# Two plain groups of the feed-forward network ahead of the products, single PSUM banks, and modulation sums in the plain chunks

## The chip, the cores and the metric

One core of one Trainium2 chip runs the program; nothing is shared with other cores. The metric is device time in microseconds, median of the runs. TensorE is written as PE, VectorE as DVE, ScalarE as ACT, GpSimd as POOL and SyncE as SP.

## The reference, cut to what matters

The program runs two blocks of two layers each. Every layer ends with a gated feed-forward network (FFN) between a modulation and a residual add:

```python
def swiglu(h, w_in, w_out):
    g, u = jnp.split(h @ w_in, 2, axis=-1)
    return (jax.nn.silu(g) * u) @ w_out
...
mod = silu_c @ ada_w[l] + ada_b[l]          # shifts, scales and gates of a layer
...
h = h + g2 * swiglu(modulate(h, norm2_g[l], sh2, sc2), ffn_w_in[l], ffn_w_out[l])
```

The model width is 1024, the hidden width 2816, which is 22 chunks of 128. In the first layer of each block the 512 tokens of the sequence and the 256 of the context go through the FFN together: 768 columns. All is float32. The modulation vectors of the second layer (`silu_c @ ada_w[1]`) depend on no activation, so they can be summed at any time before that layer.

## The kernel before

**Numbers.** TensorE multiplies in a rounded float32 format, so each operand is kept as a high part and a low part, and each product is three matmuls: high x high, high x low, low x high (`mm3`, lines 307, 309, 311, and `mmh`, lines 357 to 359). The high part is a cast on ACT, the low part a subtraction: for weights on POOL (line 300 for 1024 columns, line 349 for 512), for activations mostly on DVE (line 336 in `split`).

**The FFN over 768 tokens** (`ffn`, called in the first layer of each block; the second layers use `ffn_plain`, which the diff does not touch). It goes over the hidden chunks in groups (`FGROUPS[0]`: nine groups of two, then one of four).

- The group of chunks 0 and 1 is computed plainly: gate and up of a chunk are eight mm3 each over 768 columns into a PSUM tile `pd` of 1024 columns, of which there are three. The first three of these (gate 0, up 0, gate 1) run over the operands as they are modulated (lines 597, 598 and 578).
- The other 20 chunks (`pair`) are computed by 7 products of half width (384 columns) instead of 8, in the manner of Strassen's method: sums of halves of the operand (`half_sums`, lines 389 to 394, with casts on line 376 and low parts on line 377, made once, in `hid` tiles and with the halves of x overwritten) and sums of halves of the weights (lines 779 to 782), with the seven results combined by adds (line 770) out of PSUM tiles `sb`, of which there are four, one bank each.
- The down projection of a group (`down`) runs as a generator between the products of the next group. Each of its eight blocks of output rows goes into `sf`, a PSUM tile of 1024 columns of which there is one, in two segments of 512 and 256 columns; `residual_add` (line 642, DVE) scales each segment and adds it to `h`. The next block waits for both.
- `down_last` takes the last group of four.

**Modulation sums** (`ada`). A step is one DMA of 512 KB (a `wraw` tile, of which there are four, shared with the weights) and one or two `scalar_tensor_tensor` on DVE (line 440) that multiply it with a condition vector and accumulate; the first 16 of 48 steps have two. The one that writes its product to `junk` comes first, a second one writes over `wraw`. `fill.pace()` takes 1.3 steps at each call after a pause of five calls, so 45 steps are spread over the chunks, and `down_last` drains the other three.

**Order.** Each engine runs its instructions in the order in which they are placed, and SP issues nearly all DMAs in the same way. The code above sets the order in which work is written; a list scheduler moves it within limits on each engine.

## Time and profile before

| | us |
|---|---|
| median of 3 runs | 4068.76 (4065.93 to 4074.28) |
| profiled execution | 4067.65 |
| its span | 4065.9 |
| PE busy | 3624.0 (89%) |
| DVE busy | 2675.9 (66%) |
| ACT busy | 1455.8 (36%) |
| POOL busy | 1675.6 (41%) |

The profile is one execution. Times of rows are counted in microseconds from the start of its span. A matmul's duration includes the time that it overlaps with its neighbours, so the distance of two starts is what one costs. A wait is read from the idle time of an engine ahead of an instruction and the event that ended it. [...]

### The profile page before, as it was taken

Reading aid. Unit: us, or ns where it says so; the run is one execution under the profiler, and the core shown is the slowest. Engines: PE = TensorE matmul, PEld = TensorE weight load, DVE = VectorE, ACT = ScalarE, POOL = GpSimd, SP = SyncE. Lnnn points to the kernel's source line nnn. Section 1 sums busy time; section 2 is a strip of 40 time slices with the busy share of each in tenths; the row PEclk is TensorE's granted clock in tenths of the full one; section 3 lists DMA queues with packets and bytes.
Section 4 is the critical chain, followed back from the end, with each engine's and each line's share of the span. In section 5 each row is a group of like instructions: output and inputs, shape, how many; then the busy total and the mean of one; then the engine's idle time right before and its main releaser. Section 6 shows DMA issues by size and latency. Waiting matters only on the chain. (4 is left out here: it accounts for less than half of the span.)

```text
span 4065.9 us, 57730 instructions
## 1 busy us (share of the span) xinstructions
PE 3624.0 (89%) x22329; PEld 3065.1 (75%) x22329; DVE 2675.9 (66%) x4827; ACT 1455.8 (36%) x2609; POOL 1675.6 (41%) x1024
## 2 busy tenths in 40 slices
PE   6989889999789899988977879679999899989997
PEld 4777778998677777877756667578898777778886
DVE  4784588877776677746767654778887754464225
ACT  4542222223366322233332322332222355543222
POOL 2112355655322444432332225565555642245443
PEclk9999989999899999989986869889999899999998
DMA  5124123434111255424545767213333322122231
GB/s 193 37 95 157 45 72 110 135 125 137 57 30 45 93 171 176 153 89 120 141 130 158 233 184 260 81 32 114 120 125 121 99 67 65 60 73 78 94 99 57
DMA packets 263010, 450.21 MB, mean 111 GB/s; under 512 B 63504, under 2 KB 168592, under 8 KB 259664
## 3 DMA queue, kind: packets, MB, share of 16 engines
q1 hardware_dynamic: 257536, 424.50, 33.3%
q10 hardware_dynamic: 5200, 22.02, 1.6%
q8 instruction: 176, 2.88, 0.3%
q14 instruction: 98, 0.80, 0.1%
HBM read 383.02 MB, written 63.44 MB: 110 GB/s over the span
## 5 line engine op out<-in xcount | busy, mean ns | idle before, releaser
L300 POOL TENSOR_TENSOR wlo<-wraw,whi 128x1024 fp32r<-128x1024 f32 (+2 forms) x326 | 740.8, 2274 | 1362.3 <-ACT whi L299 1253.0
L307 PE MATMUL pd<-s,whi 128*128 128x512 f32 (+1 forms) x1881 | 644.5, 370 | 38.0 <-ACT s L577 9.5
L299 ACT CAST whi<-wraw 128x1024 fp32r<-128x1024 f32 (+2 forms) x334 | 321.4, 964 | 989.3 <-PE pd L309 471.6
L309 PE MATMUL pd<-s,whi 128*128 128x512 f32 (+1 forms) x1821 | 628.2, 369 | 14.6 <-DVE s L578 6.2
L311 PE MATMUL pd<-s,wlo 128*128 128x512 f32 (+1 forms) x1881 | 637.9, 365 | 1.6 <-POOL wlo L300 1.6
L349 POOL TENSOR_TENSOR wlo<-wraw,whi 128x512 fp32r<-128x512 f32 x240 | 377.9, 1591 | 264.9 <-ACT whi L348 264.9
L307 PEld LDWEIGHTS pd<-s,whi 128*128 128x128 f32 x1881 | 341.6, 194 | 104.2 <-issue 14.0
L357 PE MATMUL sb<-s,whi 128*128 128x384 f32 x1120 | 378.3, 338 | 15.1 <-ACT s L376 11.9
L309 PEld LDWEIGHTS pd<-s,whi 128*128 128x128 f32 x1821 | 332.6, 193 | 74.5 <-DVE s L578 10.1
L358 PE MATMUL sb<-s,whi 128*128 128x384 f32 x1120 | 378.3, 338 | 10.8 <-DVE s L377 6.2
L311 PEld LDWEIGHTS pd<-s,wlo 128*128 128x128 f32 x1881 | 342.4, 193 | 56.1 <-POOL wlo L300 3.5
L359 PE MATMUL sb<-s,wlo 128*128 128x384 f32 x1120 | 376.8, 336 | 0.0
L440 DVE SCALAR_TENSOR_TENSOR junk<-wraw,cond 128x1024 bf16<-128x1024 f32 x160 | 275.0, 1719 | 112.8 <-DMA wraw<-in_ada_w 112.3
L348 ACT CAST whi<-wraw 128x512 fp32r<-128x512 f32 x240 | 139.6, 618 | 409.3 <-PE sb L358 299.6
L357 PEld LDWEIGHTS sb<-s,whi 128*128 128x128 f32 x1120 | 212.2, 190 | 25.1 <-ACT s L376 14.3
L358 PEld LDWEIGHTS sb<-s,whi 128*128 128x128 f32 x1120 | 211.9, 189 | 15.4 <-DVE s L377 9.4
L359 PEld LDWEIGHTS sb<-s,wlo 128*128 128x128 f32 x1120 | 211.8, 189 | 0.0
L307 PE MATMUL sf<-hid,whi 128*128 128x512 f32 x576 | 154.8, 349 | 50.9 <-DVE h L642 50.9
L1149 DVE TENSOR_REDUCE negm<-sc 128x1 f32<-128x512 f32 (+1 forms) x128 | 96.1, 754 | 117.3 <-PE sc L1330 106.5
L642 DVE SCALAR_TENSOR_TENSOR h<-sf,mod,h 128x512 f32<-128x512 f32 (+1 forms) x288 | 163.7, 607 | 10.8 <-PE sf L311 10.8
L642 DVE SCALAR_TENSOR_TENSOR h<-pd,mod,h 128x512 f32<-128x512 f32 (+1 forms) x163 | 105.3, 658 | 89.0 <-PE pd L311 88.7
L309 PE MATMUL sf<-hid,whi 128*128 128x512 f32 x576 | 150.7, 342 | 1.8 <-DVE hid L336 1.8
(414 smaller groups left out, 7886.1 us busy)
## 6 DMA issues: line engine op xcount, KB each, us to landing
wraw<-in_ada_w SPq DMA_DIRECT2D x160, 512.0 KB, 3.5
wraw<-in_ffn_w SPq DMA_DIRECT2D x132, 512.0 KB, 3.5
wraw<-in_ffn_w_in SPq DMA_DIRECT2D x88, 512.0 KB, 3.5
wraw<-in_ffn_w_out SPq DMA_DIRECT2D x44, 512.0 KB, 3.6
recd<-xr SPq DMA_DIRECT2D x72, 256.0 KB, 2.9
rec<-recd ACTq DMA_DIRECT2D x12, 1536.0 KB, 7.9
rec<-recd SPq DMA_DIRECT2D x12, 1536.0 KB, 7.0
raw<-in_ada_w SPq DMA_DIRECT2D x32, 512.0 KB, 5.8
```

Of the source, the lines that this page charges most:

```text
L299: nc.scalar.copy(hi, raw)
L300: (lo_eng or nc.gpsimd).tensor_tensor(out=lo, in0=raw, in1=hi.bitcast(F32), op=ALU.subtract)
L307: nc.tensor.matmul(ps[:, o:o + b - a], lhsT=whi, rhs=xhi[:, a:b], start=start, stop=False)
L309: nc.tensor.matmul(ps[:, o:o + b - a], lhsT=whi, rhs=xlo[:, a:b], start=False, stop=False)
L311: nc.tensor.matmul(ps[:, o:o + b - a], lhsT=wlo, rhs=xhi[:, a:b], start=False, stop=stop)
L348: nc.scalar.copy(hi[:, r], src)
L349: nc.gpsimd.tensor_tensor(out=lo[:, r], in0=src, in1=hi[:, r].bitcast(F32), op=ALU.subtract)
L357: mm(ps, lhsT=hi[:, k], rhs=a, start=i == 0, stop=False)
L358: mm(ps, lhsT=hi[:, k], rhs=b, start=False, stop=False)
L359: mm(ps, lhsT=lo[:, k], rhs=a, start=False, stop=i == 3)
L440: nc.vector.scalar_tensor_tensor(raw if r else self.junk, raw, 1.0, self.cond[r], op0=ALU.mult, op1=ALU.mult, accum_out=m[:, j, r:r + 1])
L642: nc.vector.scalar_tensor_tensor(h[k][:, x:y], ps[:, x - o:y - o], m[:, g + k, r:r + 1], h[k][:, x:y], op0=ALU.mult, op1=ALU.add)
```

## The change

- Two groups are computed plainly, chunks 0 to 3. The down projection of group 0 is drained after chunk 2, with its blocks in `pd` tiles, one tile for each segment; that of group 1 runs between the first products.
- `half_sums` is called after chunk 1; its last part, which overwrites halves of x (operands `t3`), is split off into `rest()`, called after the plain chunks.
- Modulation steps: four after each of chunks 1, 2 and 3, two at every second block of the plain down, so 20 steps with 36 sums ahead of the products; then one at every second block of the later downs. `pair` has none and `down_last` none left.
- PSUM for the products is three `sb` tiles and three `sf` tiles of one bank each. A block of the down projection takes one `sf` tile for 512 columns and one for 256, each with six matmuls in a row and an evacuation of its own.
- In `pair` the low part of `hid` is computed on POOL (line 802) instead of DVE; the high part stays on ACT (line 801).

Lines move by two or more: 440 is 442 after, 578 is 580, 597 and 598 are 599 and 600, 642 is 644, 770 is 773, 779 to 782 are 782 to 785, 794 and 795 are 797 and 798, 810 is 815 (the plain chunk's product of silu and up).

```diff
--- before.py
+++ after.py
@@ -399,9 +399,11 @@
             ops["t1"].append(put(half(), y1[:, a], G))
             ops["t4"].append(put(half(), y2[:, a], V))
             t3.append((h1, l1, t))
-        for i, (h1, l1, t) in enumerate(t3):
-            ops["t3"].append(put((h1[:, b], l1[:, b]), t, (V, G)[i % 2]))
-        return ops
+        def rest():
+            for i, (h1, l1, t) in enumerate(t3):
+                ops["t3"].append(put((h1[:, b], l1[:, b]), t, (V, G)[i % 2]))
+
+        return ops, rest
 
 
     def ada_start(self, l, block):
@@ -703,7 +705,7 @@
         es = self.es
         hp = es.enter_context(self.tc.tile_pool(name=self.nm("hid"), bufs=8, reuse_waits="tile"))
         sp = es.enter_context(self.tc.tile_pool(name=self.nm("half"), bufs=1, reuse_waits="tile"))
-        BUFS.update(hid=8, s3=1, up=1, sb=4, sf=1)
+        BUFS.update(hid=8, s3=1, up=1, sb=3, sf=3)
         H = n // 2
         ha, hb = slice(0, H), slice(H, n)
         oi = 0
@@ -716,7 +718,7 @@
             done(f, ps, a, b)
             st.add(h[f], a, b)
 
-        def down(hid):
+        def down(hid, tag="sf", pace=1):
 
             nonlocal oi
             nk = len(hid)
@@ -726,12 +728,13 @@
                 hl = self.wload(wo(oi))
                 oi += 1
                 for f in range(nf):
-                    ps = self.ps("sf")
-                    for kc in range(nk):
-                        self.mm3(ps, *hl[f * nk + kc], xs[0][kc], xs[1][kc], kc == 0, kc == nk - 1, self.segs(n))
-                    done(f0 + f, ps, 0, n)
-                    if f == nf - 1:
-                        fill.pace()
+                    for a, b, o in self.segs(n):
+                        ps = self.t(self.pp, [P, 1024 if tag == "pd" else 512], tag)
+                        for kc in range(nk):
+                            self.mm3(ps, *hl[f * nk + kc], xs[0][kc], xs[1][kc], kc == 0, kc == nk - 1, [(a, b, 0)])
+                        self.residual_add(h, ps, f0 + f, m, g, a, b, o)
+                    if f % 2:
+                        fill.step(pace)
                     yield
 
         def down_last(hid):
@@ -793,27 +796,35 @@
             add(sl[:, hb], sl[:, hb], product(g2, "b2"))
             A.activation(sl, sl, AF.Silu)
             V.tensor_tensor(out=sl, in0=sl, in1=up, op=ALU.mult)
-            fill.pace()
             between.step()
-            return self.split(sl, n, pool=hp)
-
+            hi, lo = (self.t(hp, [P, T], "hid", F32R)[:, :n] for _ in range(2))
+            A.copy(hi, sl)
+            nc.gpsimd.tensor_tensor(out=lo, in0=sl, in1=hi.bitcast(F32), op=ALU.subtract)
+            return hi, lo
+
+        hids = [[], []]
         with ExitStack() as e1:
             self.psum(e1, pd=3)
             first = self.chunks([wg(0), wu(0), wg(1)], x, n, parts=parts or self.parts(n))
             self.flush()
-            hid = []
-            for c in range(2):
-                pg = first[2 * c]
+            for c in range(4):
+                pg = first[2 * c] if c < 2 else self.chunk(wg(c), x, n)
                 pu = first[1] if c == 0 else self.chunk(wu(c), x, n)
                 sl = self.s()
                 nc.scalar.activation(sl[:, :n], pg[:, :n], AF.Silu)
                 nc.vector.tensor_tensor(out=sl[:, :n], in0=sl[:, :n], in1=pu[:, :n], op=ALU.mult)
-                hid.append(self.split(sl, n, pool=hp))
-                fill.pace()
-        ops = self.half_sums(x, n, hp)
+                hids[c // 2].append(self.split(sl, n, pool=hp))
+                if c == 1:
+                    ops, rest = self.half_sums(x, n, hp)
+                if c:
+                    fill.step(4)
+                if c == 2:
+                    Fill(down(hids[0], "pd", 2)).drain()
+        rest()
+        hid = hids[1]
         with ExitStack() as e2:
-            self.psum(e2, sb=4, sf=1)
-            for grp in FGROUPS[0][1:]:
+            self.psum(e2, sb=3, sf=3)
+            for grp in FGROUPS[0][2:]:
                 between = Fill(down(hid))
                 hid = [pair(c, between) for c in grp]
                 between.drain()
```

DVE while the operands of the first FFN are modulated, before:

```order
L597 TENSOR_TENSOR s_3947<-h_3569,s_3504 128x512
L514 SCALAR_TENSOR_TENSOR st_r_3993<-rs_t_3996,st_r_3993 128x2
L598 TENSOR_SCALAR s_3947<-s_3947,modA_3817,mod_23_112 128x512
L578 TENSOR_TENSOR s_3951<-s_3947,s_3950 128x512
L597 TENSOR_TENSOR s_3954<-h_3632,s_3504 128x512
L598 TENSOR_SCALAR s_3954<-s_3954,modA_3817,mod_23_112 128x512
L597 TENSOR_TENSOR s_3961<-h_3695,s_3504 128x512
L598 TENSOR_SCALAR s_3961<-s_3961,modA_3817,mod_23_112 128x512
L578 TENSOR_TENSOR s_3965<-s_3961,s_3964 128x512
L597 TENSOR_TENSOR s_3968<-h_3746,s_3504 128x512
L598 TENSOR_SCALAR s_3968<-s_3968,modA_3817,mod_23_112 128x512
L597 TENSOR_TENSOR s_3975<-h_3778,s_3504 128x512
```

and after, with sums of line 442 between the modulation (599, 600) and the product (580) that PE multiplies:

```order
L442 SCALAR_TENSOR_TENSOR junk_419,mod_831_4055<-wraw_4378,cond_413 128x1024
L515 TENSOR_TENSOR rs_t_3996<-rs_t_3996,rs_h_3995 128x2
L599 TENSOR_TENSOR s_3947<-h_3569,s_3504 128x512
L516 SCALAR_TENSOR_TENSOR st_r_3993<-rs_t_3996,st_r_3993 128x2
L442 SCALAR_TENSOR_TENSOR wraw_4378,mod_831_4055<-wraw_4378,cond_416 128x1024
L514 TENSOR_TENSOR rs_t_3996<-st_r_3993 128x2
L600 TENSOR_SCALAR s_3947<-s_3947,modA_3817,mod_23_112 128x512
L515 TENSOR_TENSOR rs_t_3996<-rs_t_3996,rs_h_3995 128x2
L442 SCALAR_TENSOR_TENSOR junk_419,mod_831_4055<-wraw_4382,cond_413 128x1024
L516 SCALAR_TENSOR_TENSOR st_r_3993<-rs_t_3996,st_r_3993 128x2
L580 TENSOR_TENSOR s_3951<-s_3947,s_3950 128x512
L599 TENSOR_TENSOR s_3954<-h_3632,s_3504 128x512
```

In the whole stretch there are 12 such sums ahead of the last line 580 in the first FFN, and 4 in the second.

ACT at the end of the half sums, before (after the casts comes the first copy out of a product):

```order
L376 CAST s_3950<-hid_4338 128x384
L376 CAST s_4345<-hid_4337 128x384
L376 CAST s_4351<-hid_4337 128x384
L376 CAST s_4365<-hid_4355 128x384
L777 COPY s_4388<-sb_4389 128x384
L376 CAST s_3957<-hid_4338 128x384
L376 CAST s_4351<-hid_4356 128x384
L376 CAST s_4365<-hid_4356 128x384
```

and after, where the silu of chunk 2's gate (line 814, `pd_4392`) stands behind the casts of line 376:

```order
L376 CAST s_4315<-hid_4320 128x384
L376 CAST s_4344<-hid_4335 128x384
L376 CAST s_4329<-hid_4320 128x384
L376 CAST s_4344<-hid_4336 128x384
L376 CAST s_4350<-hid_4336 128x384
L376 CAST s_4364<-hid_4354 128x384
L814 ACTIVATE s_4496<-pd_4392 128x768
L376 CAST s_4350<-hid_4355 128x384
L335 CAST hid_4499<-s_4496 128x768
```

The silu was not there before, since chunk 2 was made by products. The third tile of the plain down takes the buffer of chunk 2's up, which DVE's line 815 reads; that comes after the two lines 644 of the first block.

POOL at the end of a group, before:

```order
L300 TENSOR_TENSOR wlo_6119<-wraw_6116,whi_6118 128x1024
L349 TENSOR_TENSOR wlo_6139<-wraw_6072,whi_6138 128x512
L349 TENSOR_TENSOR wlo_6139<-s_1122_6076,whi_6138 128x512
L349 TENSOR_TENSOR wlo_6189<-wraw_6073,whi_6188 128x512 x2
L349 TENSOR_TENSOR wlo_6239<-wraw_6072,whi_6238 128x512
```

and after, with the low part of the group's second `hid` behind the down weights (line 300) and two parts of the next chunk's weights:

```order
L300 TENSOR_TENSOR wlo_6161<-wraw_6158,whi_6160 128x1024
L349 TENSOR_TENSOR wlo_6182<-wraw_6114,whi_6181 128x512
L349 TENSOR_TENSOR wlo_6182<-s_1150_6118,whi_6181 128x512
L802 TENSOR_TENSOR hid_6111<-s_5907,hid_6110 128x768
L349 TENSOR_TENSOR wlo_6236<-wraw_6115,whi_6235 128x512 x2
L349 TENSOR_TENSOR wlo_6287<-wraw_6114,whi_6286 128x512
```

The low part of `hid`, which stood on DVE, now stands behind three instructions of POOL; for the first chunk of a group it stands behind the down weights alone.

## Rows read from the trace of the kernel before

**Rows 1.** The page, engine totals: busy us, share of the span, instructions.
```profile
PE 3624.0 (89%) x22329; PEld 3065.1 (75%) x22329; DVE 2675.9 (66%) x4827; ACT 1455.8 (36%) x2609; POOL 1675.6 (41%) x1024
```

**Rows 2.** Stretches by line 357, first FFN: us, busy (instructions), clock, DMA.
```profile
574.20:626.50 52.30, 19.04 (x56) 10.79 (x57) 0.97 0.35 111
...
731.70:779.50 47.80, 18.75 (x56) 10.54 (x57) 1.00 0.42 133
...
971.00:1002.40 31.40, 18.84 (x56) 10.50 (x56) 1.00 0.53 163
```

**Rows 3.** The same, second FFN.
```profile
2757.50:2809.00 51.50, 18.73 (x56) 10.49 (x57) 1.00 0.34 113
...
3154.00:3184.20 30.20, 18.71 (x56) 10.48 (x56) 1.00 0.52 159
```

**Rows 4.** PE's waits, 574 to 1002: total us, times, longest.
```profile
PE sf L307 <- DVE h L642: 19.8, 18, 2.5
```

**Rows 5.** Stretches, all engines: PE, PEld, DVE, ACT, POOL busy, clock, DMA.
```profile
503.00:534.00 31.00, 18.28 (x67) 14.12 (x67) 25.94 (x30) 9.46 (x19) 21.06 (x13) 0.67 0.05 17
...
574.00:731.00 157.00, 144.19 (x790) 134.76 (x789) 136.82 (x189) 42.52 (x66) 86.17 (x48) 0.97 0.36 114
```

**Rows 6.** PE's waits, 503 to 537.
```profile
PE sb L357 <- ACT s L376: 7.6, 2, 4.8
PE sb L358 <- POOL s L377: 2.3, 2, 1.7
```

**Rows 7.** Timeline, PE: start, duration, engine, line, tiles, count.
```profile
497.69 0.51 PE L307 MATMUL pd<-s,whi 128*128 128x512 f32 x2
...
498.74 0.51 PE L307 MATMUL pd<-s,whi 128*128 128x512 f32 x2
...
822.24 0.34 PE L357 MATMUL sb<-s,whi 128*128 128x384 f32 x1
...
822.76 0.33 PE L357 MATMUL sb<-s,whi 128*128 128x384 f32 x1
```

**Rows 8.** Line 440, 400 to 1040: ns minimum/median/maximum, first and last start.
```profile
L440 DVE SCALAR_TENSOR_TENSOR junk<-wraw,cond x48: 1208/1226/2317, 546.9 to 988.9; 128x1024 bf16<-128x1024 f32 x48
...
L440 DVE SCALAR_TENSOR_TENSOR wraw<-wraw,cond x16: 1211/1842/2355, 548.5 to 711.9; 128x1024 f32<-128x1024 f32 x16
```

**Rows 9.** Timeline, DVE, half sums.
```profile
503.10 0.95 DVE L810 TENSOR_TENSOR s<-s,pd 128x768 f32<-128x768 f32 x1 [2.13 <-PE pd L311]
...
510.75 0.94 DVE L390 TENSOR_TENSOR hid<-s,s 128x768 f32<-128x768 f32 x1
...
529.73 1.35 DVE L391 TENSOR_TENSOR hid<-hid 128x384 f32<-128x384 f32 x1
```

**Rows 10.** Timeline, all engines, end of a group.
```profile
823.92 1.13 DVE L642 SCALAR_TENSOR_TENSOR h<-sf,mod,h 128x512 f32<-128x512 f32 x2
...
824.15 0.34 PE L359 MATMUL sb<-s,wlo 128*128 128x384 f32 x1
...
825.11 0.61 PE L307 MATMUL sf<-hid,whi 128*128 128x512 f32 x2 [0.62 <-DVE h L642]
825.51 2.94 POOL L300 TENSOR_TENSOR wlo<-wraw,whi 128x1024 fp32r<-128x1024 f32 x1 [3.13 <-ACT whi L299]
...
828.41 2.02 POOL L349 TENSOR_TENSOR wlo<-wraw,whi 128x512 fp32r<-128x512 f32 x1
...
829.30 0.84 ACT L335 CAST hid<-s 128x768 fp32r<-128x768 f32 x1 [0.73 <-DVE s L795]
...
830.38 2.01 POOL L349 TENSOR_TENSOR wlo<-s,whi 128x512 fp32r<-128x512 f32 x1
...
831.52 0.51 PE L307 MATMUL sf<-hid,whi 128*128 128x512 f32 x2
```

**Rows 11.** POOL's sum of operand parts, line 389: ns minimum/median/maximum.
```profile
L389 POOL TENSOR_TENSOR hid<-s,s x4: 1832/2032/2293, 505.9 to 527.4; 128x768 f32<-128x768 f32 x4
```

## The prediction

> **What bounds the kernel now.** I read the page's engine totals first: TensorE is busy 89% of the span [rows 1], so over the whole program only matmul work or idle TensorE time can move the end. The diff touches the two feed-forward networks over 768 tokens (about 455 to 1002 us, and 2640 to 3184 us), so I cut these into stretches by the matmuls of the 7 products, 28 of the first kind to a chunk. [...] In the first network a group of two chunks takes 52.3 us at first and 47.8 us later [rows 2]; the second starts at 51.5 [rows 3]. The table of waits says what is idle: from 574 to 1002 us `sf` waits 19.8 us for line 642, the residual add that empties its only buffer [rows 4]. In the early groups VectorE is the late one: busy 136.8 of 157 us [rows 5]. [...]
>
> **The change part by part, matmul work.** In the plain chunk three pairs (512 + 256 columns) take 498.74 - 497.69 = 1.05 us, and 16 such triples make a chunk: 16.7 us. Three matmuls of a product take 822.76 - 822.24 = 0.52, so a product of 12 is 2.08 and a chunk of 7 is 14.6 [rows 7]. Two more plain chunks in each network therefore cost 4.2 us each, 8.4 in all; this is inside the walk below. The comparison stands where the same work is left, the last 18 chunks by products: before at 574.2 and 2757.5 us.
>
> **The plain part, first network.** A modulation sum takes 1.23 us (median) in the form that writes `junk`, 1.84 in the one that writes `wraw` and 1.21 at best, with 0.08 for the accumulator [rows 8]; I take 1.31 each. The order puts 12 of them among the modulation of the operands ahead of its last product (line 578, now 580), where VectorE works nearly without a gap before. 12 x 1.31 = 15.7; two weight sums of 0.68 leave the place, four gaps of 0.69 behind ScalarE are filled, and about a microsecond of slack goes: +10.5. What stood at 503.1 us (the last plain product, [rows 9]) comes at 513.6. Then silu x up, one sum and the low part: the half sums start at 518.5. TensorE has the new chunk 2 (16.7 us) and the first down tile to do, until 531.5.
>
> Here the order makes a new wait. The down projection of group 0 goes through the three `pd` buffers, two of which hold gate and up of chunk 2. The second down tile needs the gate's buffer, freed by ScalarE's silu, which is queued behind the casts of the half sums; these wait for VectorE's line 391 of the last quarter. Before, from the first line 390 to the end of that line 391 is 510.75 to 531.1 = 20.3 us [rows 9], of which 1.9 is work of others; now four sums (5.2) and an evacuation (0.7) stand in it: 24.4, so 542.9, and with the silu 543.8. TensorE idles 12 us at the second tile, and 2.4 more at the third, which needs the up buffer behind two VectorE steps. The rest of the down is VectorE's: 7 evacuation pairs of 1.13 [rows 10], 3 us of half sums, a low part and four sums are 17.8, to 565.5. The weights of chunk 3 share the ring of four with the modulation loads and follow VectorE's sums: I put 3 us on it, about two sums. Chunk 3 is 16.7, its first columns at a lower clock 2: the products start at 588, **14 us later** than 574.2. Meanwhile eight more sums (10.5) lie under chunk 3 and cost nothing; without that cover they would be 10.5.
>
> Bounds: if TensorE never waits in the down, it is 12 + 2.4 earlier, so 0; if every sum takes 1.84 as in the slower form, the some 20 on this path add 0.6 each, so 26. In the second network the order has only 4 sums ahead of line 580, but 8 instead of 4 among the evacuations: the first term falls from 10.5 to some 0 to 4, the last grows by 5: **+9** (bounds -3 and 21).
>
> **The stretch by products.** Late groups of 47.7 still hold some 0.62 us of wait per chunk (as [rows 10] show at 825.11), so without any they are 46.4. Eight groups of 46.4 and the last two chunks at 29.5 (14.6 each, and the gaps between) are 400.7, where before 574.2 to 1002.4 is 428.2 [rows 2] and 2757.5 to 3184.2 is 426.7 [rows 3]: a gain of 27.5 + 26 = 53.5. Three reasons let me take it whole: a buffer is free when the third last tile is emptied; the 32 steps of one sum each come to 28, one to every second block; and the low part of `hid` leaves VectorE.
>
> But the low part goes to GpSimd, and there it costs. Before, at a group's end, the last product ends at 824.5; GpSimd does the next down weights (825.51, 2.94) and two weight parts (828.41, 830.38), to 832.4; `hid` hi starts on ScalarE at 829.30 and its low part on VectorE is done before `sf` starts at 831.52 [rows 10]. Now line 802 stands behind those two weight parts. GpSimd's nearest operation, two inputs of 768 columns, takes 1.83 to 2.29, median 2.03 [rows 11]: it would end at 834.4, 9.9 after the last product. TensorE has an `sf` pair and two products in between (6.25) and 0.92 of the new `sf` until it reads that part: at 7.2. If all four operations run at their shortest, it lands 0.7 late, with these durations 2.7. I take 1.8, since VectorE, which is busy beside GpSimd, has less to do. Seven downs in each network follow a group's end so: 14 x 1.8 = 25 (bounds 10 and 38). For first chunks of a group there is slack of a whole chunk: nothing.
>
> The split evacuations cost VectorE the same 512 + 256; six 512-column matmuls before six of 256 instead of alternating cost TensorE under 0.12 a chunk, in the 46.4. Clock lost after the longer holes: an estimate of 3 in all (the clock was 0.67 in such a stretch, [rows 5]), bounds 0 and 8.
>
> **Sum**, against the profiled 4067.65 us (span 4065.9; the median is 1.1 higher): +14 + 9 - 53.5 + 25 + 3 = -2.5, so 4065 beside that run, **4067 us** beside the median of 4068.76. It is a change of no size that comes from two terms of 25 to 50.
>
> **The rivals.** *Hidden backlog.* ScalarE's casts come early enough, so the second down tile finds its buffer: the half sums are through by 531. For it speaks that some of the half-sum chain was waiting for GpSimd (line 377, [rows 6]), into which sums fall free. Against it, VectorE was busy 25.9 of 31 us [rows 5]. It would save 14 in each network: 4039. *Low part on time.* If GpSimd's weight parts run ahead, the 25 are not lost: 4042. For it, GpSimd idles 3 us ahead of the down weights at 825.51 [rows 10]; against it, it waits there for ScalarE's cast, which stays where it is.
>
> *Sums at the slow rate* (slower). The sum that writes `wraw` has 1.21 at best and 1.84 in the middle, 2.36 at worst [rows 8], with the same size: something beside it slows it, and GpSimd is the engine that is busy 21 of 31 us there [rows 5]. If the some 20 sums on the path take 1.84 + 0.08 instead of 1.31, each network loses 12: 4091. It decides from a mean of 1.6 in the plain part. [...]
>
> *Banks that free nothing* (slower). If the early `sf` waits are VectorE's lateness and not the single buffer, three small banks only put them off: a bank holds one segment, so three hold 1.5 of the old tiles. Half of the 53.5 would go: 4094. Against it, the early groups shrink from 52.3 to 47.8 us once the steps carry one sum [rows 2], with one buffer all the while.
>
> **How the numbers follow.** My forecast has 0.36 (own range 4056 to 4078), hidden backlog 0.20, low part on time 0.12, slow sums 0.22, banks that free nothing 0.10. A measurement of this kernel tells about 0.2% from no change, that is 4060.6 to 4076.9. Faster: 0.20 + 0.12 + 0.05 of the forecast's lower end = 0.37; within: 0.28; slower: 0.22 + 0.10 + 0.03 = 0.35. The range 4038 to 4096 leaves out both gains together, and slow sums together with a low part 2.7 late.
>
> **What would show it.** In the profile after: the first product of chunk 4 at about 588 and 2767 us; a wait of `pd` for ScalarE's silu of some 12 us in each down of group 0; `sf` waiting for line 802 some 1 to 3 us, 14 times, and hardly for line 644; groups of two chunks at 46.4 to 48.5 from the first on; and some 36 modulation sums at a mean near 1.3 us ahead of the first product. The forecast is wrong if the wait for the silu is missing, or if line 802 is never waited for (both faster), or if the sums' mean passes 1.6 or `sf` still waits for VectorE (both slower).

## The result, and the profile after

| | before | after |
|---|---|---|
| median, us | 4067.98 (4 runs, 4065.93 to 4074.28) | 4115.67 (4 runs, 4112.12 to 4120.63) |
| span of the profiled execution, us | 4065.9 | 4114.3 |

The ratio is 1.0115, 95% interval 1.0098 to 1.0133: the change makes the kernel 48 us slower. The forecast was 4067 with a range of 4038 to 4096.

The page of the changed kernel has the engine totals (beside [rows 1]) and, among the costliest groups, a wait that did not exist before (columns: busy and mean ns | idle before it and what ended it):

```profile
PE 3646.1 (89%) x22377; PEld 3082.9 (75%) x22377; DVE 2607.7 (63%) x4747; ACT 1443.5 (35%) x2585; POOL 1683.8 (41%) x1040
...
L309 PE MATMUL sf<-hid,whi 128*128 128x512 f32 (+1 forms) x512 | 175.6, 343 | 30.1 <-POOL hid L802 30.1
```

DVE has 68 us less to do, and PE 22 us more. 30.1 us of idle PE end with POOL's line 802.

**Where the time went.** The stretches of the first network by products, all engines (us; busy PE, PEld, DVE, ACT, POOL; granted clock as a share of full speed):

```profile
596.70:644.70 48.00, 47.99 (x264) 45.40 (x265) 29.30 (x47) 12.02 (x19) 21.17 (x16) 0.97 0.37 110
...
696.50:748.30 51.80, 48.39 (x267) 45.24 (x266) 34.43 (x50) 13.79 (x22) 27.72 (x19) 0.97 0.32 102
...
898.40:946.60 48.20, 46.43 (x267) 43.85 (x266) 30.72 (x47) 15.71 (x24) 28.70 (x19) 1.00 0.34 110
```

And of both networks by line 357 alone, the last two chunks and, in the second, the first group (us; PE, PEld; clock):

```profile
994.20:1029.30 35.10, 19.58 (x56) 10.87 (x56) 0.95 0.25 76
...
2801.20:2849.20 48.00, 19.64 (x57) 11.20 (x57) 0.96 0.33 110
...
3199.10:3234.20 35.10, 19.44 (x56) 10.84 (x56) 0.95 0.26 76
```

The bounds of these stretches are the account, beside [rows 2, 3]. The 18 chunks by products start at 596.7 instead of 574.2 us: **+22.5**. They last 1029.3 - 596.7 = 432.6 instead of 428.2: **+4.4**. From there to the second start it is 1771.9 instead of 1755.1: **+16.8**. The second stretch is 433.0 instead of 426.7: **+6.3**, and what follows -1.6. Together 48.4, the difference of the spans. The +16.8 hides more: it holds 6.4 us that the code between the two networks was shorter. From the matmul that ends PE's wait for the modulation's statistics in the second network (2639.92 before, 2660.40 after) to the first product it is 140.8 instead of 117.6, **+23.2**.

**The plain part.** PE's waits from 500 to 600 us, beside [rows 6]:

```profile
PE pd L307 <- DVE h L644: 16.1, 2, 14.2
PE sb L357 <- DVE s L815: 7.0, 1, 7.0
```

The timeline of DVE, with the one row of PE that waits longest, ACT's silu and SP's load of the weights of the first products, beside [rows 9]:

```profile
520.97 0.94 DVE L815 TENSOR_TENSOR s<-s,pd 128x768 f32<-128x768 f32 x1
...
524.64 0.95 DVE L390 TENSOR_TENSOR hid<-s,s 128x768 f32<-128x768 f32 x1
...
545.03 0.74 DVE L644 SCALAR_TENSOR_TENSOR h<-pd,mod,h 128x512 f32<-128x512 f32 x1
...
545.83 0.58 PE L307 MATMUL pd<-hid,whi 128*128 128x256 f32 x1 [14.21 <-DVE h L644]
...
548.88 0.80 ACT L814 ACTIVATE s<-pd 128x768 f32<-128x768 f32 x1
...
576.47 1.22 DVE L442 SCALAR_TENSOR_TENSOR junk<-wraw,cond 128x1024 bf16<-128x1024 f32 x1
...
577.72 0.33 SPq L767 DMA_DIRECT2D wraw<-in_ffn_w_in  x1
...
585.12 1.19 DVE L782 TENSOR_TENSOR s<-wraw,wraw 128x512 f32<-128x512 f32 x1 [1.65 <-DMA wraw<-in_ffn_w_in]
...
593.41 2.28 DVE L442 SCALAR_TENSOR_TENSOR junk<-wraw,cond 128x1024 bf16<-128x1024 f32 x1
...
595.62 0.94 DVE L815 TENSOR_TENSOR s<-s,pd 128x768 f32<-128x768 f32 x1
```

The last plain product of chunk 1 comes at 520.97 (503.10 before), the half sums start at 524.64 (510.75), the second tile of the plain down starts at 545.83 after 14.2 us of nothing, and the first product waits 7.0 us for line 815 of chunk 3. On DVE a sum stands ahead of that line, and ahead of the sum the weight sums of the first products (lines 782 to 785), which start only at 585.12. Their load was issued at 577.72, right after the sum of 576.47, since both kinds of loads share the ring of four; in the run without sums in this part (e5, below) it was issued at 504.59. The sums in this part, grouped by line (busy us, mean ns), and then those of the first network before the change:

```profile
L442 DVE SCALAR_TENSOR_TENSOR junk<-wraw,cond 128x1024 bf16<-128x1024 f32 x22 | 34.7, 1578 | 4.7 <-DMA wraw<-in_ada_w 4.7
L442 DVE SCALAR_TENSOR_TENSOR wraw<-wraw,cond 128x1024 f32<-128x1024 f32 x16 | 28.2, 1764 | 0.2
```

```profile
L440 DVE SCALAR_TENSOR_TENSOR junk<-wraw,cond 128x1024 bf16<-128x1024 f32 x48 | 73.5, 1532 | 16.1 <-DMA wraw<-in_ada_w 16.1
...
L440 DVE SCALAR_TENSOR_TENSOR wraw<-wraw,cond 128x1024 f32<-128x1024 f32 x16 | 27.8, 1740 | 0.3
```

62.9 us in 38 sums are 1.66 each (1.58 in the second network), where [rows 8] gave medians of 1.23 and 1.84. The 64 sums before the change took 101.3 us, a mean of 1.58: the sums hardly became slower.

**The end of a group**, beside [rows 10], timeline of all engines:

```profile
849.39 2.89 POOL L300 TENSOR_TENSOR wlo<-wraw,whi 128x1024 fp32r<-128x1024 f32 x1 [3.18 <-ACT whi L299]
...
852.24 2.00 POOL L349 TENSOR_TENSOR wlo<-wraw,whi 128x512 fp32r<-128x512 f32 x1
...
853.13 0.84 ACT L801 CAST hid<-s 128x768 fp32r<-128x768 f32 x1 [0.73 <-DVE s L798]
...
854.21 1.29 POOL L349 TENSOR_TENSOR wlo<-s,whi 128x512 fp32r<-128x512 f32 x1
...
854.47 0.39 PE L307 MATMUL sf<-hid,whi 128*128 128x512 f32 x1
...
855.46 1.80 POOL L802 TENSOR_TENSOR hid<-s,hid 128x768 fp32r<-128x768 f32 x1
...
857.32 0.50 PE L309 MATMUL sf<-hid,whi 128*128 128x512 f32 x1 [1.76 <-POOL hid L802]
```

The high part is ready at 853.97, but POOL turns to the low part at 855.46, behind three instructions, and PE, which got to the new down at 854.47, stands from 855.56 to 857.32.

### The profile page after: what moved, and what is told of

The parts are those of the page before. It is cut to its first block, busy times and chain, and to the rows that moved or that the text cites. A ratio compares the mean times of both kernels' runs of the same rounds, so it can differ in the third digit from the quotient of the medians.

```text
span 4114.3 us, 57753 instructions
## 1 busy us (share of the span) xinstructions
PE 3646.1 (89%) x22377; PEld 3082.9 (75%) x22377; DVE 2607.7 (63%) x4747; ACT 1443.5 (35%) x2585; POOL 1683.8 (41%) x1040
## 5 line engine op out<-in xcount | busy, mean ns | idle before, releaser
L307 PE MATMUL pd<-s,whi 128*128 128x512 f32 (+1 forms) x2009 | 681.6, 371 | 45.3 <-ACT s L579 13.3
L309 PE MATMUL pd<-s,whi 128*128 128x512 f32 (+1 forms) x1949 | 665.9, 369 | 19.2 <-POOL s L580 10.0
L311 PE MATMUL pd<-s,wlo 128*128 128x512 f32 (+1 forms) x2009 | 675.7, 366 | 4.4 <-POOL wlo L300 4.4
L307 PEld LDWEIGHTS pd<-s,whi 128*128 128x128 f32 x2009 | 364.0, 195 | 117.0 <-ACT s L579 17.8
L309 PEld LDWEIGHTS pd<-s,whi 128*128 128x128 f32 x1949 | 355.7, 195 | 83.5 <-POOL s L580 14.8
L349 POOL TENSOR_TENSOR wlo<-wraw,whi 128x512 fp32r<-128x512 f32 x216 | 312.0, 1461 | 248.4 <-ACT whi L348 238.2
L357 PE MATMUL sb<-s,whi 128*128 128x384 f32 x1008 | 345.0, 342 | 24.1 <-DVE s L815 15.5
L358 PE MATMUL sb<-s,whi 128*128 128x384 f32 x1008 | 344.5, 342 | 0.0
L359 PE MATMUL sb<-s,wlo 128*128 128x384 f32 x1008 | 343.2, 341 | 0.0
L357 PEld LDWEIGHTS sb<-s,whi 128*128 128x128 f32 x1008 | 194.8, 193 | 25.8 <-issue 18.4
L309 PE MATMUL sf<-hid,whi 128*128 128x512 f32 (+1 forms) x512 | 175.6, 343 | 30.1 <-POOL hid L802 30.1
L358 PEld LDWEIGHTS sb<-s,whi 128*128 128x128 f32 x1008 | 194.3, 193 | 0.0
L307 PE MATMUL pd<-hid,whi 128*128 128x512 f32 (+1 forms) x432 | 153.2, 361 | 40.0 <-DVE h L644 37.8
L307 PE MATMUL sf<-hid,whi 128*128 128x512 f32 (+1 forms) x512 | 173.9, 340 | 3.8 <-ACT hid L801 3.5
L311 PE MATMUL sf<-hid,wlo 128*128 128x512 f32 (+1 forms) x512 | 175.7, 343 | 0.0
```

What stands on the lines that cost most here:

```text
L307: nc.tensor.matmul(ps[:, o:o + b - a], lhsT=whi, rhs=xhi[:, a:b], start=start, stop=False)
L309: nc.tensor.matmul(ps[:, o:o + b - a], lhsT=whi, rhs=xlo[:, a:b], start=False, stop=False)
L311: nc.tensor.matmul(ps[:, o:o + b - a], lhsT=wlo, rhs=xhi[:, a:b], start=False, stop=stop)
L349: nc.gpsimd.tensor_tensor(out=lo[:, r], in0=src, in1=hi[:, r].bitcast(F32), op=ALU.subtract)
L357: mm(ps, lhsT=hi[:, k], rhs=a, start=i == 0, stop=False)
L358: mm(ps, lhsT=hi[:, k], rhs=b, start=False, stop=False)
```

## The experiments

Medians are of the runs beside runs of the kernel before on the same chip; ratios are to that kernel. The kernel before itself came to 4062 to 4068 us in these rounds, so differences between rounds are good to a few us, and the ratios are the safer measure.

| label | median, us | ratio, 95% interval |
|---|---|---|
| e1_lo_vector | 4068.74 | 1.0005 (0.9994 to 1.0016) |
| e2_no_sums_ahead | 4105.06 | 1.0086 (1.0053 to 1.0120) |
| e3_banks_alone | 4087.44 | 1.0053 (1.0034 to 1.0073) |
| e4_lo_gpsimd_alone | 4101.46 | 1.0078 (1.0052 to 1.0103) |
| e5_sums_even | 4076.40 | 1.0031 (1.0018 to 1.0045) |
| e6_lo_split | 4104.21 | 1.0097 (1.0078 to 1.0117) |
| e7_one_group_even | 4094.96 | 1.0074 (1.0049 to 1.0098) |
| e8_silu_early | 4068.94 | 1.0013 (0.9997 to 1.0029) |
| e9_changed_later_block | 4080.06 | 1.0032 (1.0019 to 1.0045) |
| e10_silu_later_block | 4062.33 | 0.9992 (0.9979 to 1.0005) |
| e11_silu_later_block_lo_gpsimd | 4093.11 | 1.0069 (1.0042 to 1.0097) |
| e12_banks_later_block | 4069.54 | 1.0007 (0.9989 to 1.0025) |
| e13_sums_behind_operands | 4043.18 | 0.9952 (0.9933 to 0.9972) |
| e14_sums_behind_half_sums | 4048.94 | 0.9963 (0.9950 to 0.9977) |

### The low part on VectorE again

```diff
-            hi, lo = (self.t(hp, [P, T], "hid", F32R)[:, :n] for _ in range(2))
-            A.copy(hi, sl)
-            nc.gpsimd.tensor_tensor(out=lo, in0=sl, in1=hi.bitcast(F32), op=ALU.subtract)
-            return hi, lo
+            return self.split(sl, n, pool=hp)
```

> The changed kernel with one part undone: the low part of hid in the product chunks is computed on VectorE again (line 336), as before. Theory (the low part on GpSimd is what ate the gain of the banks): the 14 waits of sf for line 802 go (30.1 us in the profile of the changed kernel), the wait of some 3.4 us near the end of each network goes, and the low clock that follows the longer waits (a group at 51.8 us where PE at full clock needs 46.4) goes with them: 4065 us, at most 4080. Rival (VectorE is the late engine all along, GpSimd only took the wait over): sf then waits for line 336 or 644 instead, the groups stay near 50 us, and the time is 4100 to 4116.

Measured 47 us below the changed kernel (45 by the ratios), level with the kernel before. Three stretches of the first network (columns as above), then PE's waits from 600 to 1030 us:

```profile
593.80:642.50 48.70, 48.70 (x264) 46.24 (x265) 32.87 (x48) 12.00 (x19) 21.16 (x16) 0.95 0.36 108
...
738.60:784.70 46.10, 46.10 (x267) 43.86 (x266) 35.49 (x51) 13.91 (x22) 27.09 (x17) 1.00 0.38 115
...
971.80:1004.30 32.50, 30.50 (x175) 29.80 (x174) 18.89 (x24) 12.80 (x19) 21.81 (x14) 1.00 0.30 90
```

```profile
PE sf L307 <- ACT hid L335: 1.9, 3, 0.6
PE sb L357 <- DVE s L773: 1.8, 2, 1.3
PE sf L309 <- DVE hid L336: 1.8, 3, 0.6
```

The 14 waits are gone, groups take 46.1 us, so the stretch is 1004.3 - 593.8 = 410.5 us: 22.1 less than with the low part on GpSimd, and 17.7 less than before the change. The theory holds; what is left is the late start in each network (593.8 us in the first), which eats the gain of the stretches.

### No sums ahead of the products

```diff
-        def down(hid, tag="sf", pace=1):
+        def down(hid, tag="sf", pace=2):
...
-                if c:
-                    fill.step(4)
...
-                    Fill(down(hids[0], "pd", 2)).drain()
+                    Fill(down(hids[0], "pd", 0)).drain()
```

> The changed kernel with no modulation sums in the plain chunks: all 48 steps go with the later down projections, two at every second block. Theory (the sums ahead of the products are on VectorE's path): the operands are ready some 10 us earlier in the first network, the half sums some 6 us more, the first product does not wait 7 to 8.6 us for line 815; the products start some 20 us earlier in the first network and 14 in the second. The first four groups by products then carry 16 sums each, so VectorE fills to 49 of 52 us and sf waits for it a little: 4085 to 4095 us. Rival (the plain part is bound by the half sums and the down projection, the sums lie beside): 4105 to 4120 us.

The products start at 568.2 us, 28.5 earlier than in the changed kernel and 6 earlier than before the change, so the second plain group by itself gains. But the sums come back where they go: with two steps at every second block the second group takes

```profile
619.00:677.70 58.70, 50.82 (x267) 46.35 (x266) 52.86 (x76) 14.94 (x24) 35.48 (x19) 0.94 0.42 136
```

DVE is busy 52.9 of 58.7 us. Net 11 us below the changed kernel, which four runs from 4092 to 4115 do not tell from nothing, above the theory's 4085 to 4095 and at the foot of the rival's range. The start was worth more than the theory had (28.5 us, not 20), the sums by products cost more.

### One part of the change alone

The banks, on the kernel before:

```diff
-        BUFS.update(hid=8, s3=1, up=1, sb=4, sf=1)
+        BUFS.update(hid=8, s3=1, up=1, sb=3, sf=3)
...
-                    ps = self.ps("sf")
+                    for a, b, o in self.segs(n):
+                        ps = self.t(self.pp, [P, 512], "sf")
```

> The kernel before with one part of the change alone: three sb and three sf tiles of a single bank, each segment of a down block with its own tile and evacuation. Everything else as before (one plain group, sums paced, low part on VectorE). Theory (the single sf buffer makes the waits): of 42 us of sf waits in the two networks nearly all go, late groups fall from 47.8 to 46.4 us, early ones from 52.4 to 48 or 49: 4040 us. Rival (VectorE is late, the buffer count moves nothing): early groups stay above 51 us and the time is 4060 to 4068 us.

Both theories are wrong: it is 21 us slower. PE's waits from 570 to 1012 us, where [rows 4] had 19.8 us for line 642:

```profile
PE sf L309 <- DVE hid L336: 15.1, 7, 4.0
PE sb L357 <- DVE s L771: 11.4, 8, 3.3
PE sf L307 <- DVE h L642: 1.6, 3, 0.9
```

The waits for the residual add are gone (1.6 us left), and the low part of `hid` and the adds of the products are late instead. Waiting for the single buffer had given the chain behind a group's last product (add, silu, product, high part, low part) the time that it needs; e12 below tests this.

The low part on GpSimd, on the kernel before (the diff of e1 the other way round):

> The kernel before with one part of the change alone: the low part of hid in the product chunks on GpSimd. Theory (it comes late at each group's end): a wait of 2 to 3 us for GpSimd at 8 group ends in each network, with some low clock behind it, against 1.6 us per chunk that VectorE gains in the early groups: 4080 to 4095 us. Rival (harmless where VectorE is the late engine): 4055 to 4068 us.

4101 is above the expected 4080 to 4095, 36 us slower than before: eight waits for the low part in the first network (10.1 us in all), and the waits for line 642 stay at 27.4.

### Sums spread evenly

e1 without sums in the plain part; one step at every second block in the first four downs, two in the last four:

```diff
-                between = Fill(down(hid))
+                between = Fill(down(hid, pace=1 if i < 4 else 2))
```

> The changed kernel with two parts undone: the low part of hid on VectorE, and no modulation sums in the plain chunks; the 48 steps go evenly with the later down projections, one at every second block in the first four (two sums each), two in the last four (one sum each), so 8 sums to a group. Theory (the two costs add, and 8 sums to a group fit VectorE): the products start at 568 us as in the run without sums ahead, groups take 46.4 to 47.5 us as in the run with the low part on VectorE: 976 instead of 1002 us at the end of the first network, the same gain in the second, 4010 to 4025 us. Rival (VectorE cannot hold 8 sums and the low part in a group): sf waits for line 336 as in the kernel with the banks alone, groups of 49 to 50 us, 4050 to 4065 us.

The start is 567.0 us as expected, but groups take 48 to 54 us: the rival, and the time is beyond even its 4050 to 4065. The end of a group, timelines of DVE, POOL and PE:

```profile
870.65 2.94 DVE L442 SCALAR_TENSOR_TENSOR junk<-wraw,cond 128x1024 bf16<-128x1024 f32 x1
...
877.34 2.04 DVE L442 SCALAR_TENSOR_TENSOR junk<-wraw,cond 128x1024 bf16<-128x1024 f32 x1 [1.01 <-DMA wraw<-in_ada_w]
...
879.32 2.00 DVE L336 TENSOR_TENSOR hid<-s,hid 128x768 fp32r<-128x768 f32 x1
```

```profile
870.11 2.39 POOL L300 TENSOR_TENSOR wlo<-wraw,whi 128x1024 fp32r<-128x1024 f32 x1 [4.16 <-ACT whi L299]
```

```profile
881.38 0.79 PE L309 MATMUL sf<-hid,whi 128*128 128x512 f32 x1 [4.01 <-DVE hid L336]
```

Two sums stand in the chain, one ahead of the last add, one ahead of the low part and itself waiting for its load, and PE waits 4.0 us. In e1 there is at most one.

The low part on GpSimd for a group's first chunk only:

> As the kernel with even sums, but the low part of hid on GpSimd for the first chunk of each group, and on VectorE for the second. Theory (GpSimd's low part hurts only where the next down reads it at once, at the group's end): no wait of sf for GpSimd, and VectorE has 1.6 us less per group: same as the kernel with even sums or up to 10 us faster. Rival (any low part on GpSimd delays weight parts behind it, products wait for them): 10 to 25 us slower than the kernel with even sums, with waits for line 349 or 300.

28 us slower than e5, as the rival's size, but not for its reason: waits for line 349 are 4.1 us, and those for VectorE's line 336 rose from 15.3 to 25.9 in the first network. In the profiles the two stretches by products are 28.3 us longer than in e5, of which 16.0 are idle PE and 12.3 the same matmuls kept busy longer (mean granted clock of the profiled execution 0.935, in e5 0.936). Why line 336 came later is not settled.

The kernel before with the banks and even sums, one plain group:

> The kernel before (one plain group, low part on VectorE, half sums undivided) with the single banks, and with the 48 steps evenly in the downs as in the kernel with even sums, none in the plain chunks or behind the silu of a product chunk. Theory (banks alone cost time because steps placed at the end of a product chunk stood ahead of the low part on VectorE): sf no longer waits for line 336, groups 46.4 to 47.5 us, the stretch of 18 chunks starts at 570 to 574 us: 4015 to 4030 us. Rival (three sb banks instead of four make products wait for the adds, line 771): waits of some 10 us per network for those adds stay, 4060 to 4080 us.

Neither: 18.3 us wait for line 336 and 6.5 for line 771, so moving the sums alone does not bring the low part forward.

Chunk 2's silu ahead of the casts (e5, with gate, up and their product of chunk 2 written ahead of `half_sums`):

```diff
+                    two = gated(2)
                     ops, rest = self.half_sums(x, n, hp)
```

> As the kernel with even sums, but chunk 2's gate, up, silu and their product are written ahead of the half sums, so the silu stands ahead of the casts on ScalarE. Theory (the second tile of the plain down waits for a silu that is queued behind casts): the wait of 10.4 us for line 814 goes, part of it comes back as a wait for VectorE's product or evacuations: the products start 4 to 8 us earlier in each network, 8 to 16 us in all against the kernel with even sums. Rival (the half sums on VectorE bound the plain down, the silu's place only shows it): same time within 5 us.

The start moves from 567.0 to 561.5 us, so the queue on ScalarE cost 5.5 there; the medians differ by 7.5, with overlapping intervals. That is just under the theory's 8 to 16 and beyond the rival's 5. (The profiled execution of e8, 4054.98, is the second fastest of its ten.)

### The next down's first block later

Three kernels (e9 on the changed kernel, e10 on e8, e12 on e3), and e11, which is e10 with the low part on GpSimd:

```diff
-            between.step()
+            if not lead:
+                between.step()
...
-                hid = [pair(c, between) for c in grp]
+                hid = [pair(c, between, c == grp[0]) for c in grp]
```

> The changed kernel with only the place of the down projection's blocks moved: the first block of a group's down is written two products later, behind the fourth product of the next group's first chunk instead of the second, and the last block is drained behind the group. So 4.2 us more of products and one more block (2.1 us) lie between a group's last product and the first matmul that reads its low part. Theory (the low part on GpSimd is late by 1.3 to 2.8 us only because the next down follows 6.25 us after the group's last product): all 14 waits of sf for line 802 go, and the low clock behind them: 4068 to 4080 us. Rival (the low part on GpSimd also holds up the weight parts behind it): products wait for line 349, 4095 to 4115 us.

36 us below the changed kernel, with no wait for line 803 (802 of the change) left: only the distance made the low part late. The last 11 us to e1 stay; products wait 10.1 us for VectorE's adds (line 773) in the first network, where e1 has 1.8.

> As the kernel with the silu early and even sums (low part on VectorE), with the same later place of the down's blocks. Theory (in the kernels with even sums the sums that stand ahead of the low part on VectorE expose a chain that has no slack at a group's end): sf no longer waits for line 336, groups of 46.4 to 48 us instead of 48.5 to 54: 4005 to 4025 us. Rival (VectorE has too much to do with 8 sums in a group, wherever they stand): waits for line 644 or 773 take their place, 4050 to 4070 us.

6.6 us below e8, not 50: the rival. Line 336 is waited for no more; line 644 is (17.1 us in the first network), and so is the low part of the down weights (line 300, 9.0), beside a DVE with eight sums to a group.

> As the kernel before this one, with the low part of hid on GpSimd as in the change. Theory (with slack at the group's end the engine of the low part does not matter, VectorE has 3.2 us less in a group): within 8 us of it, on either side. Rival (GpSimd is the slower place even with slack): 20 us or more slower, with waits for weight parts.

31 us above e10, which neither theory has by its mechanism: waits for line 349 are 0.6 us, those for the down weights (line 300) 11.4 instead of 9.0, those of products for DVE's adds 13.0 instead of 6.7, and those for line 644 11.7 instead of 17.1. The profiled execution, the fastest of its four, has 22.8 us more in the two stretches than e10's: 7.3 are idle PE, and 15.5 the same matmuls kept busy longer (mean granted clock of the profiled execution 0.943, in e10 0.944). Why they took longer here, and why GpSimd is dearer than in e9, stays open.

> The kernel before with single banks alone, and the down's blocks later in the same way (one plain group, sums paced as before, low part on VectorE). Theory (the banks lost 21 us because PE came to the down's first block before the low part was there): the 16.5 us of waits for line 336 in the first network go and their low clock with them: 4030 to 4050 us. Rival (three sb banks are the loss): the waits of products for line 771, 11 us a network, stay or grow: 4070 to 4090 us.

18 us below e3, level with the kernel before, and above the theory's 4030 to 4050. No wait for line 336 is left. An early and a late group:

```profile
621.90:675.50 53.60, 48.40 (x266) 44.80 (x266) 42.89 (x63) 14.04 (x22) 27.10 (x16) 0.98 0.34 105
...
822.00:868.10 46.10, 46.10 (x266) 43.81 (x265) 34.00 (x54) 14.11 (x23) 25.35 (x16) 1.00 0.40 126
```

Two late groups have no wait at all, the next takes 49.2 us; the groups with two sums to a step are longer than before (52.3, [rows 2]), and products still wait 9.1 us for the adds (line 771), against 0.9 with four banks. In e1, with the same three `sb` banks, products wait only 1.8 us for the adds in the whole stretch, so three banks need not cost. No run has four of them beside small `sf` ones.

### Which sums cost in the plain part

On e8: twelve steps in the plain part, of which the scheduler puts none ahead of the operands, and one step at every second block later.

```diff
-                    Fill(down(hids[0], "pd", 0)).drain()
+                    Fill(down(hids[0], "pd", 2)).drain()
+                if c == 3:
+                    fill.step(4)
...
-                between = Fill(down(hid, pace=1 if i < 4 else 2))
+                between = Fill(down(hid, pace=1))
```

> The kernel with the silu early (low part on VectorE), with 12 of the 48 steps in the plain part, eight in the plain down projection and four after chunk 3, so that none of their sums stands ahead of the last modulated operand; the other 36 at every second block of the later downs, one step each. Theory (sums cost in the plain part mainly where they stand ahead of the operands and of the half sums, and four sums to a group cost nothing by products): products start at 575 to 580 us in the first network where the kernel with the low part on VectorE had 593.8, groups at 46.1 to 47.9 us but the first, 4030 to 4045 us. Rival (any sum in the plain part is on VectorE's path, wherever it stands): products start at 588 to 594 us, 4055 to 4070 us.

> As the kernel before this one, with all 12 steps after chunk 3, of which the scheduler puts 4 sums among the half sums and 15 between these and chunk 3's product of silu and up. Theory: six sums fewer ahead of the half sums bring the start another 2 to 5 us forward, if the first product then does not wait longer for line 815 of chunk 3: 4025 to 4045 us. Rival: the first product waits for that line, which stands behind 15 sums (20 us), start at 580 to 585 us, 4045 to 4060 us.

e13 starts its products at 573.8 us, 20.0 ahead of e1. It has the early silu too, worth 5.5 in e8; if it is worth the same here, which no run shows, the other 14.5 are the sums (24 instead of 36, none ahead of the operands). e14, with `fill.step(12)` after chunk 3 and none in the plain down, starts at 574.3: the sums ahead of the half sums cost no more than those behind them. The first two groups of e13:

```profile
573.80:631.10 57.30, 49.95 (x267) 45.14 (x266) 54.24 (x70) 15.62 (x24) 33.14 (x19) 0.97 0.35 120
631.10:677.30 46.20, 46.20 (x265) 43.73 (x265) 34.56 (x48) 13.73 (x22) 25.76 (x17) 1.00 0.36 115
```

Most of the price is paid by the first group, with DVE busy 54.2 of 57.3 us. Both kernels beat the kernel before, e13 by 0.5%, which is 1.6% below the change.

## Why the prediction was wrong

The mechanisms were there; three terms of the sum were mis-sized, all in the same direction.

**The plain part**: +14 and +9 forecast, +22.5 and +16.8 measured, or +23.2 for the second when the shorter code ahead of it is left out, which is beyond the bound of 21. The walk held up to the operands: PE takes up chunk 1's up at 503.4 us, 10.5 later than the 492.9 of before. Then a sum took 1.66 + 0.08, not 1.31: seven of them between the operands and chunk 1's last product took 15.7 us instead of 9.2, and the half sums start at 524.6, not 518.5. The rival of slow sums, whose border was 1.6, came true in the first network and just missed it in the second (1.58); but I had it as a thing that the change might bring, where the mean before the change was 1.58 already and I had priced with the median. The second tile did wait, 14.2 us instead of 12, but not for the silu: it starts as the first tile's evacuation ends, which stands behind the same half sums and sums on DVE (the silu runs three us later, and the third tile waits after it for another evacuation). So at the second tile only 2.0 us are lost against the walk (545.83, not 543.8), and PE is through with chunk 3 at 589.75, 43.9 later, where the walk had 44.2 to the first product. That agreement is partly luck, since the steps as written do not add up: 565.5 + 3 + 16.7 + 2 is 587.2, not 588, and between 543.8 and 565.5 lie 1.5 us that no term names. The 2 in it, for chunk 3's first columns at a lower clock, was my estimate, which no row showed; in the profile after, the clock is 0.50 from 570.94 to 576.0 us and 1.00 from 576.1 to the chunk's end. The rest of the miss is the cover, where I had costed eight sums at nothing: the first product waits 7.0 us (8.6 in the second network) for line 815, behind weight sums whose load came late through the ring and a modulation sum. I had named the price without cover, 10.5, and not put any of it in. e13 and e14, with fewer sums and none ahead of the operands, start 20 us earlier than e1.

**The stretch without waits**: 53.5 forecast, 17.7 + 19.6 = 37.3 measured in e1. Groups do come down to 46.1, but the first takes 48.7 and the last two chunks 32.5 instead of 29.5. (e1 has the low part on VectorE; the forecast counted on its leaving.) e3 shows what the reasoning lacked: the rival "banks that free nothing" was right that the banks alone bring no gain, though not for its reason, since the waits for line 642 did vanish. That wait was not idle time to be had; it covered the chain behind a group's last product, which became the next late thing.

**The low part on GpSimd**: 25 forecast, 22.1 + 25.9 = 48 measured (stretches of the changed kernel against e1: 432.6 against 410.5, and 433.0 against 407.1). The 14 waits are 14.8 + 15.3 = 30.1, 2.15 each, within the bounds of 0.7 to 2.7 (the longest 2.8). The rest is mostly longer busy time of PE, in the stretches of the changed kernel and then of e1 (us; PE; clock):

```profile
596.70:1029.30 432.60, 411.27 (x2280) 0.98 0.32 99
2801.20:3234.20 433.00, 410.72 (x2280) 0.98 0.31 98
```

```profile
593.80:1004.30 410.50, 404.23 (x2285) 0.99 0.33 105
2776.10:3183.20 407.10, 402.02 (x2286) 1.00 0.34 105
```

The same matmuls keep PE busy 822.0 us instead of 806.3: 15.7 of the 48 are that, at a granted clock of 0.98 in both stretches instead of 0.99 and 1.00. I had put a lower clock at 3 for everything, with a bound of 8. The other 32.3 are idle PE, the 30.1 among them. Three short stretches of the changed kernel, right behind waits of 2.75, 1.78 and 1.76 us (columns as above, all engines):

```profile
705.40:709.00 3.60, 3.57 (x13) 3.43 (x14) 3.23 (x4) 0.00 (x0) 3.35 (x2) 0.55 0.00 0
...
806.80:810.40 3.60, 3.60 (x16) 3.51 (x17) 3.19 (x4) 0.00 (x0) 3.31 (x2) 0.69 0.02 5
...
857.30:861.00 3.70, 3.68 (x22) 3.60 (x23) 3.25 (x5) 0.00 (x0) 3.35 (x2) 1.00 0.02 4
```

Behind the first the granted clock was 0.55 for 3.6 us, so a wait of 2.75 cost some 4.4, an estimate (2.75 + 0.45 x 3.6); behind the third it was 1.00. Here the length of a wait did not decide alone: behind 1.78 us the clock was 0.69, behind 1.76 us 1.00. The early groups, 51.8 to 50.6 us, have a mean clock of 0.97, the late ones, 48.2 to 47.6, of 1.00.

Of the signs I named, the waits for line 802, the missing waits for line 644 and the long wait in the plain down came, the last of them without the silu as its cause, which I had called a sign of a faster kernel; the start was 9 us later than the 588 I gave, and groups of 46.4 appeared only with the low part back on VectorE.

## What to carry to other kernels

A wait that a second buffer removes may be the slack of a chain that nothing shows as late: before giving the buffer, time that chain against the new moment at which its result is read. Work moved from a busy engine to an idle one is priced by the queue that it joins, not by its own duration, and by the clock that PE can lose behind a wait (here 0.55 for 3.6 us behind one of 2.75, and none behind one of 1.76). Many instructions of one kind are priced by their mean, not by their median. Filler work belongs behind the operands that the bound engine is about to read, and where it is counted as covered, the instruction that stands behind it in the queue, and the load that waits for its buffer, are to be named.

## What the runs showed of the hardware

**Modulation sums on VectorE and instructions of GpSimd mostly waited for each other's end.** In the profile after, a modulation sum takes 1.22 us, or up to 3.45 when it starts while GpSimd is at work. Timelines of POOL and DVE:

```profile
514.45 2.71 POOL L300 TENSOR_TENSOR wlo<-wraw,whi 128x1024 fp32r<-128x1024 f32 x1 [2.85 <-ACT whi L299]
```

```profile
513.68 1.22 DVE L442 SCALAR_TENSOR_TENSOR junk<-wraw,cond 128x1024 bf16<-128x1024 f32 x1
...
515.00 3.25 DVE L442 SCALAR_TENSOR_TENSOR wraw<-wraw,cond 128x1024 f32<-128x1024 f32 x1
```

The sum at 513.68 was running when POOL's instruction started and took its usual 1.22; POOL's ended 2.26 us after it, close to the 2.34 to 2.40 that such an instruction takes where VectorE does nothing (33 of them); all 35 of line 300 of this size that start while a sum runs end 2.20 to 2.35 us after that sum. The one at 515.00 started while POOL's ran until 517.16, and ended 1.09 later, at 518.25, as if it had begun only then. The same in e5: POOL until 872.50, the sum from 870.65 until 873.59. Of the 256 sums in the whole profile after, 139 meet no instruction of POOL and 37 start ahead of one: all 176 take 1.19 to 1.23 us. 80 start while one of POOL runs, and 74 of these end 1.07 to 1.17 us after its end. So the median of 1.23 and the mean of 1.66 come from two populations, and here the price of such a sum was its own time plus, in 74 of 256 cases, the rest of the instruction that POOL was at. This is the mechanism of the rival of slow sums. By it a low part moved to GpSimd can hold up a sum for up to 1.84 us (the median of line 802), an estimate from these rows that no run isolates: in the profile after no sum overlaps an instruction of line 802.
